# Layer 0's input projection: its last 18 column tiles in nine seven-product pairs behind the attention, and conditioning sums 1024 columns wide

## The chip, the cores and the metric

The kernel runs on one core of one Trainium2 chip. The metric is device time in microseconds (us): the median of three runs of the kernel before is 2300.96 us (2299.42 to 2301.28). One more execution was profiled; all rows shown come from it. Engine names as in the profile: PE is TensorE's matmul, PEld its weight load, DVE is VectorE, ACT is ScalarE, POOL is GpSimd, SP is SyncE, which issues most transfers.

## The reference, cut to what matters

Two transformer layers on 640 tokens (512 latent, 128 context), width 2048, all fp32. Per layer: a conditioning vector (shift, scale, gate) from a small matrix product, RMSNorm, one input projection, mixers, one output projection, gated residual.

```
m = silu(cond) @ ada_w[l] + ada_b[l]           # for c and for c_ctx: two rows, 2048 x 6144 weights
sh, sc, gt = split(m, 3)
h = rms_norm(x, norm_g[l]) * (1 + sc) + sh
# layer 0
qa, ka, va, ga, ub, bb, cb, gb = split_cols(h @ w_in)   # 1024, 256, 256, 1024, 4 x 1024 columns
y_a = banded_attention(q, k, v, sink) * silu(ga)        # 8 heads, 2 key heads
z = cb * ub
conv = zp[:, :-2] * w[0] + zp[:, 1:-1] * w[1] + zp[:, 2:] * w[2]    # depthwise, width 3
y_b = bb * conv * silu(gb)
x = x + gt * (concat([y_a, y_b]) @ w_out)
```

Layer 1 has two dense attention mixers behind its own input projection; the change touches it only through one helper and through the conditioning sums.

## The kernel before, in words

Everything is feature-major: a tile is 128 output columns of a projection by 640 tokens, held as two halves of 320 (`HALF`). The input h stays in SBUF as 16 slabs of 128 features (`hs[k]`), each split in a high and a low part, and so is each weight block (`split_w`, L239 on ACT and L240 on DVE). A product is three matmuls: high by high, high by low, low by high (`proj_q`, L274 to L276). One tile is 4 quarters of k x 2 halves x 4 slabs x 3 = 96 matmuls of 320 columns.

`run_tiles` runs a list of tiles. The first six of layer 0 are led together, while h is made; the others run one by one on two alternating PSUM pairs. Weight quarters are loaded five ahead and split three ahead. After each quarter comes a `slot`: it moves on the generators of `prep` (norms, rotations, gates of finished tiles), those of `attn` (softmax attention of a pair of heads, 11 steps) and, by a credit of `FILL0` per slot, one step of a *fill*.

The fill is `ada_on_dve`: a conditioning block is 512 columns of `ada_w`, summed over 16 blocks of 128 rows. For each, a 256 KB load comes on the SP queue and DVE does two scalar-times-tensor sums of 512 columns (L209, L211), one for each conditioning row. A last fold over the partitions goes through PE, ACT and PE (L217, L220, L223). Layer 0's list does twelve blocks this way; eight more are done on PE before (`ada_on_pe`, L176), four by layer 1's list.

Layer 0 has 52 tiles: q 8, k 2, v 2, attention gate 8, and u, b, c, h (the convolution's input, two factors and gate) 8 each. All 52 are in one list, so attention is spread over the first part of it, and the last 16 tiles are u, c, b, h.

`run_pairs` does two column tiles at once in seven products of half size instead of eight (a Strassen-Winograd form). It needs sums and differences of the halves of the moving operand (`forms`: T2, T3, T4 and T1), made once, and of the four quarters of the weights (operands M1 to M7), made for each pair on DVE. One product is 24 matmuls of 320 columns (L528 to L530). The kernel uses it in both output projections and in a part of layer 1's input projection; `project` runs some single tiles first, and in the last of them the second halves of slabs 0 to 7 are overwritten by T1.

The pools `even` (attention and its work tiles) and `mid` (forms, 8-block weights `w8`, `xr` tiles) share memory. Before, `mid` opens in the middle of the output projection's first tiles, when y is loaded back as its input. The order on each engine is made by the tile framework: it takes instructions in the order of the program as far as their inputs are ready in its own timing.

The softmax (`soft`, L705 to L718) takes the maximum on DVE, the exponential on ACT, the reciprocal on DVE; the weights are scaled on DVE (L798) and transposed on PE (L726).

Of the kernel before, what the change touches and what calls it, by code (L numbers as in the profile page):

```python
# [20 lines left out]
P = 128  # L21
# [28 lines left out]
N_FILL0 = 12  # L50
FILL0 = 1.2
# [5 lines left out]
def trunk_kernel(ctx: ExitStack, tc: tile.TileContext, I: dict, O: dict):  # L57
# [131 lines left out]
    def ada_on_dve(blocks, tags, parts=1, tie=lambda: None):  # L189


        wt, wd = tags[2:5], 512 // parts
        bufs = 3 if wt[0] == wt[1] else 1
        for l, cb in blocks:
            ap = pools["cur"]
            acc = [ap.tile([P, 512], F32, tag=tags[c], name=f"acc{c}", bufs=1) for c in range(2)]
            mark = tie()
            if mark is not None:
                for c in range(2):
                    V.tensor_copy(acc[c][:, 0:1], mark)  # L200
            for i in range(KT * parts):
                kt, h = i % KT, i // KT
                w = ap.tile([P, wd], F32, tag=wt[i % 3], name="adaw", bufs=bufs)
                c0 = cb * 512 + h * wd
                nc.sync.dma_start(w, I["ada_w"][l, kt * P:(kt + 1) * P, c0:c0 + wd])
                for c in range(2):
                    a = acc[c][:, h * wd:(h + 1) * wd]
                    if kt == 0:
                        V.tensor_scalar(a, w, sT[:, kt, c:c + 1], None, ALU.mult)  # L209
                    else:  # L210
                        V.scalar_tensor_tensor(out=a, in0=w, scalar=sT[:, kt, c:c + 1], in1=a,  # L211
                                               op0=ALU.mult, op1=ALU.add)
                yield
            s = psT()
            for g in range(4):
                c, h = g // 2, g % 2
                PE.matmul(s[32 * g:32 * g + 32, 0:256], ones, acc[c][:, h * 256:(h + 1) * 256],  # L217
                          start=True, stop=True, tile_position=(0, 32 * g))
            sb = ap.tile([P, 256], F32, tag=tags[5], name="ada_sb2", bufs=3 if tags[5] == wt[0] else 1)
            A.copy(sb, s[:, 0:256])  # L220
            t = psT()
            for j in range(2):
                PE.transpose(t[:, j * P:(j + 1) * P], sb[:, j * P:(j + 1) * P], ident)  # L223
            t = t[:, 0:256].rearrange("p (j c h x) -> p h j c x", j=2, c=2, h=2)
            for h in range(2):
                add_bias(l, cb, t[:, h, :, :, 0], 2 * h, 2)
            ada_done(l, cb)
            ready.add((l, cb))
            yield

    ready = set()

    def need(l, n, fill):
        while (l, 8 + n // 4) not in ready:
            next(fill)
# [74 lines left out]
    def run_tiles(jobs, w_ap, make_h, fill=None, rate=0.0, ahead=None, order=(0, 1, 2, 3), before=None,  # L310
                  last=None, by_half=False, trans=[], grace=0, cut=None, summed=None, led=None, fill_from=0, lead_in=None, steps=lambda i: 1.0):
# [8 lines left out]
        else:  # L320
# [3 lines left out]
               else new_pp(1 + held.index(n) if trans else n) for n in leads}  # L324
        units = [(pos, qd, js) for pos, qd in enumerate(order) for js in (cut or [(0, 4)])]
        for ui, (pos, qd, js) in enumerate(units if leads else ()):
            queue = nc.gpsimd if trans and ui else None
            raws = {n: load_raw(w_ap, jobs[n][0], qd, js, queue) for n in leads[:W_BUFS]}
            if ui == 0 and lead_in:
                lead_in()  # L330
            parts = {n: split_w(raws[n]) for n in raws}
# [68 lines left out]
        for i in range(lead, len(jobs)):  # L400
            fn = jobs[i][1]
            pp = new_pp((i - lead) % 2)
            split_last = last is not None and i == len(jobs) - 1
# [31 lines left out]
    def run_pairs(cols, w_ap, mov, room, used, begin, done, tail):  # L435
# [82 lines left out]
        for i, (p, name) in enumerate(seq):  # L518
# [25 lines left out]
            if name in ("M7", "M3") and p == len(cols) - 1:  # L544
                tail(name)
# [157 lines left out]
    def soft(ap, width, s, n, rsc, nsink=None, sink=None):  # L703
# [9 lines left out]
        if sink is not None:  # L713
            es = small.tile([P, 1], F32, tag="es", name="es")
            A.activation(es, sink, AF.Exp, bias=nm)
            V.tensor_add(l, l, es)
# [48 lines left out]
    def pair_gen(ap, width, k, v, qs, banded, begin, emit, done, sinks):  # L765
# [27 lines left out]
        def score(u, j):  # L793
            segs, masks, lo, hi, _ = plan(u)
            q = qs[j]
            s = scores(q, u, k, segs, masks)
            p, rl, _ = soft(ap, width, s[:, lo:hi], hi - lo, q[2][u], *sinks[j])
            V.tensor_scalar(p[:, 0:hi - lo], p[:, 0:hi - lo], rl, None, ALU.mult)  # L798
            ps.setdefault(u, []).append(p)
# [35 lines left out]
    ada_rest = [(0, cb) for cb in range(8, 12)] + [(1, cb) for cb in (4, 0, 5, 1, 6, 2, 7, 3, 8, 9, 10, 11)]  # L835
    fill0 = ada_on_dve(ada_rest[:N_FILL0], ("acc0", "acc1", "adaw", "adaw", "adaw", "z"))
    fill1 = ada_on_dve(ada_rest[N_FILL0:], ("acc0", "acc1", "adaw", "adaw", "adaw", "adaw"), 2,
# [125 lines left out]
    def pair_then(width, kk, i, banded, gated):  # L963

        def then():
# [14 lines left out]
            def done():  # L980
                if i in gated:
                    save_y(i, i + 1)
# [4 lines left out]
    def late_gate_job(i, load=False):  # L987
        def f(pp):
            ap = pools["cur"]
            if i < 8 and not load:  # L990
                drain(attn)
            if load and i % 2 == 0:
                y_pair(i)
                for k in (i, i + 1):
                    nc.sync.dma_start(y[k], ydram[k])
# [41 lines left out]
    jobs = []  # L1037

    def b_tiles(i):
        for n, fn in (("u", u_job), ("c", c_job(i)), ("b", b_job(i)), ("h", late_gate_job(8 + i))):  # L1040
            jobs.append((EV[n] + i * P, fn))

    for i in range(4):
        kv, h = i // 2, 2 * i
        if i % 2 == 0:
            jobs.append((EV["k"] + kv * P, k_job("k0", I["cache_a_k"][0, 0, kv], "a_k_norm", O["new_a_k"][0, 0, kv])))
            jobs.append((EV["v"] + kv * P, v_job(I["cache_a_v"][0, 0, kv], O["new_a_v"][0, 0, kv])))
        jobs.append((EV["q"] + h * P, q_job("q0", "a_q_norm")))
        jobs.append((EV["q"] + (h + 1) * P, q_job("q1", "a_q_norm", pair_then(640, "k0", h, True, gated))))
        b_tiles(i)  # L1050
        for j in (h, h + 1):
            jobs.append((EV["g"] + j * P, late_gate_job(j) if i else gate_job(j)))
    for i in range(4, 8):
        b_tiles(i)

    u0, c0, b0, h0, g0, g1 = jobs[4:10]
    jobs[0:10] = [u0, jobs[0], jobs[1], g0, jobs[2], jobs[3], g1, c0, b0, h0]
    run_tiles(jobs, I["ev_w_in"][0], h0_maker, fill0, FILL0, ada_group, trans=TRANS, grace=GRACE, cut=((0, 2), (2, 4)),
              summed=keep, led=even_start, lead_in=lambda: ada_on_pe(0, 0, 0, 2))
    drain(prep)  # L1060
    for _ in fill0:
        pass

# [10 lines left out]
    def forms(src):  # L1074
# [3 lines left out]
        def load(j):  # L1078
            ts = [big("w8", bufs=4)[:, 0:NT] for _ in range(2)]
# [6 lines left out]
        nxt = load(0)  # L1086
        for j in range(8):
            (ya, yb), nxt = nxt, (load(j + 1) if j < 7 else None)
# [18 lines left out]
    def res_load(l, n):  # L1107
        loaded.add((l, n))
        st["xr", n] = pools["cur"].tile([P, NT], F32, tag="xr", name="xr", bufs=3)
# [8 lines left out]
    def late_yin(k):  # L1118
        t = pools["cur"].tile([P, NT], F32, tag="xr", name="yin", bufs=3)
# [10 lines left out]
    def project(w, cols, n0, maker, job, begin, done, tail, n_lead=3, **kw):  # L1130

        go_on = run_tiles([(cols[n], job(n)) for n in range(n_lead)], w, maker, **{"order": (0, 2, 1, 3), **kw})
# [13 lines left out]
        for n in range(n_lead, n0):  # L1146

            used = (n - n_lead) % 2 if n_lead == 3 else 2 if n == n_lead else n % 2
# [60 lines left out]
    make_y0 = y_maker(("q0h", "q0l", "q1h", "q1l"), NT)  # L1209

    def y0_maker(k):
        if k < 4:
            return make_y0(k)
        if k == 8:
            close("even")
            open_pool("mid")
            st["acc"] = pools["cur"].tile([P, NT], F32, name="acc")
            st["sq"] = pools["cur"].tile([P, NT], F32, name="sq")
            attn.append(forms(ydram))
        late_yin(k)  # L1220
# [23 lines left out]
    def norm_half(n, h):  # L1244
# [19 lines left out]
        if h:  # L1264
            st["rbc"] = big("xr", bufs=3)
# [5 lines left out]
    def x1_tail(name):  # L1271

        for i in (range(0, 4) if name == "M7" else range(4, 6)):
# [6 lines left out]
    project_out(0, y0_maker, x1_done, x1_last, x1_tail)  # L1280
# [131 lines left out]
    def gate_out(n):  # L1412
        g = pools["cur"].tile([P, NT], F32, tag="xr", name="g", bufs=3)
# [7 lines left out]
    def value_rows(n, t):  # L1421
        yield
        r = pools["cur"].tile([P, 5, P], F32, tag="xr", name="vr", bufs=3)
# [55 lines left out]
    def very_late_gate(i):  # L1479
        def f(pp):  # L1480
            ap = pools["cur"]
            ti, t, g = (ap.tile([P, NT], F32, tag=tag, name=n, bufs=b)
                        for tag, n, b in (("rp", "yg", 3), ("stg", "gt_t", 2), ("rp", "gg", 3)))
            nc.sync.dma_start(ti, ydram[i])
            for j, sl in HV:
                A.activation(t[:, sl], pp[j][:, 0:HALF], AF.Tanh, scale=0.5)
                V.scalar_tensor_tensor(out=g[:, sl], in0=t[:, sl], scalar=1.0, in1=pp[j][:, 0:HALF],
                                       op0=ALU.add, op1=ALU.mult)
            V.tensor_mul(g, ti, g)
            nc.gpsimd.dma_start(ydram[i], g)  # L1490
        return f

# [21 lines left out]
    for i in (4, 5):  # L1514
        jobs.append((OD["cg"] + i * P, very_late_gate(i)))
# [115 lines left out]
```

## Time and profile before

| | us |
|---|---|
| median of three runs | 2300.96 |
| profiled execution | 2295.65 |
| its span, first to last instruction | 2293.9 |
| PE busy | 2254.7 |
| DVE busy | 1660.4 |
| ACT busy | 1001.3 |
| granted TensorE clock | 0.999 |

Busy is the union of an engine's instructions. A matmul's record is longer than the time to the next one, so PE's pace is read from start to start; DVE's and ACT's instructions overlap a little in the same way. In a row of a group stand the line, engine, operation, tiles out<-in, shapes and count, then busy us and mean ns of one, then the engine's idle time before them and what ended it. In a row in order of time stand the start, the length, engine, line and operation.

### The profile page before, as it was taken

Reading aid. Unit: us, or ns where it says so; the run is one execution under the profiler, and the core shown is the slowest. Engines: PE = TensorE matmul, PEld = TensorE weight load, DVE = VectorE, ACT = ScalarE, POOL = GpSimd, SP = SyncE. Lnnn points to the kernel's source line nnn. Section 1 sums busy time; section 2 is a strip of 40 time slices with the busy share of each in tenths; the row PEclk is TensorE's granted clock in tenths of the full one; section 3 lists DMA queues with packets and bytes.
Section 4 is the critical chain, followed back from the end, with each engine's and each line's share of the span. In section 5 each row is a group of like instructions: output and inputs, shape, how many; then the busy total and the mean of one; then the engine's idle time right before and its main releaser. Section 6 shows DMA issues by size and latency. Waiting matters only on the chain.

```text
span 2293.9 us, 41889 instructions
## 1 busy us (share of the span) xinstructions
PE 2254.7 (98%) x15924; PEld 2183.7 (95%) x15924; DVE 1660.4 (72%) x3327; ACT 1001.3 (44%) x2095; POOL 193.4 (8%) x267
## 2 busy tenths in 40 slices
PE   8999999999999999999999999999999999999999
PEld 5889999999999999999999999999999999999999
DVE  5669887786866663977786665868768778677665
ACT  4335432433422222544654455455555554544343
POOL 2220000000000000000100000100000111111001
PEclk9999999999999999999999999999999999999999
DMA  9984445445455543944673334413324234237541
GB/s 369 330 281 128 151 125 164 139 132 159 127 179 155 153 139 108 288 138 133 228 228 115 116 106 147 137 60 94 111 69 148 73 117 131 77 112 235 159 138 60
DMA packets 398266, 347.54 MB, mean 152 GB/s; under 512 B 19683, under 2 KB 343745, under 8 KB 397553
## 3 DMA queue, kind: packets, MB, share of 16 engines
q1 hardware_dynamic: 384704, 296.19, 42.5%
q0 software_dynamic: 12496, 46.45, 5.4%
q8 instruction: 125, 2.05, 0.4%
q10 hardware_dynamic: 864, 2.23, 0.3%
q14 instruction: 77, 0.62, 0.1%
HBM read 303.89 MB, written 40.90 MB: 150 GB/s over the span
## 4 chain that ended last, share of the span: by engine, by line
PE 85%; DVE 6%; DMA 4%; issue 2%; ACT 2%; POOL 1%; SPq 0%; POOLq 0%; ACTq 0%; DVEq 0%
PE pa L274 8%; PE pb L274 8%; PE pb L275 8%; PE pb L276 8%; PE pa L275 8%; PE pa L276 8%; PE pq L530 7%; PE pq L529 7%; PE pq L528 7%; PE T L726 2%; PE S L738 1%; PE T L176 1%; DMA adaw<-in_ada_w 1%; PE S L740 1%; PE S L739 1%
## 5 line engine op out<-in xcount | busy, mean ns | idle before, releaser
L239 ACT ACTIVATE wh<-raw 128x512 fp32r<-128x512 f32 (+1 forms) x454 | 275.7, 608 | 659.6 <-PE pb L275 546.8
L274 PE MATMUL pa<-h,wh 128*128 128x320 f32 x1504 | 477.3, 317 | 2.4 <-ACT h L239 1.8
L275 PE MATMUL pa<-h,wh 128*128 128x320 f32 x1504 | 467.2, 311 | 1.3 <-DVE h L240 1.1
L274 PE MATMUL pb<-h,wh 128*128 128x320 f32 x1504 | 466.8, 311 | 0.9 <-ACT h L239 0.9
L276 PE MATMUL pb<-h,wl 128*128 128x320 f32 x1504 | 466.5, 310 | 0.0
L276 PE MATMUL pa<-h,wl 128*128 128x320 f32 x1504 | 466.2, 310 | 0.0
L275 PE MATMUL pb<-h,wh 128*128 128x320 f32 x1504 | 465.7, 310 | 0.0
L240 DVE TENSOR_TENSOR wl<-raw,wh 128x512 fp32r<-128x512 f32 (+1 forms) x454 | 299.6, 660 | 226.2 <-ACT wh L239 210.1
L211 DVE SCALAR_TENSOR_TENSOR acc<-adaw,sT,acc 128x512 f32<-128x512 f32 (+1 forms) x600 | 359.6, 638 | 12.0 <-DMA adaw<-in_ada_w 11.6
L274 PEld LDWEIGHTS pa<-h,wh 128*128 128x128 f32 x1504 | 282.8, 188 | 13.9 <-issue 10.0
L275 PEld LDWEIGHTS pa<-h,wh 128*128 128x128 f32 x1504 | 283.1, 188 | 6.2 <-issue 3.7
L276 PEld LDWEIGHTS pa<-h,wl 128*128 128x128 f32 x1504 | 282.5, 188 | 2.9 <-issue 2.9
L274 PEld LDWEIGHTS pb<-h,wh 128*128 128x128 f32 x1504 | 283.0, 188 | 2.1 <-ACT h L239 1.1
L275 PEld LDWEIGHTS pb<-h,wh 128*128 128x128 f32 x1504 | 282.9, 188 | 0.4 <-issue 0.4
L276 PEld LDWEIGHTS pb<-h,wl 128*128 128x128 f32 x1504 | 282.9, 188 | 0.4 <-issue 0.4
L528 PE MATMUL pq<-h,wh 128*128 128x320 f32 x608 | 188.6, 310 | 0.0
L530 PE MATMUL pq<-h,wl 128*128 128x320 f32 x608 | 188.1, 309 | 0.2 <-DVE wl L240 0.2
L529 PE MATMUL pq<-h,wh 128*128 128x320 f32 x608 | 187.8, 309 | 0.0
L712 ACT ACTIVATE p<-S,nm,rq 128x768 f32<-128x768 f32 (+3 forms) x120 | 101.3, 844 | 101.1 <-DVE nm L707 69.4
L528 PE MATMUL pq<-T,wh 128*128 128x320 f32 x456 | 141.8, 311 | 0.1
L530 PE MATMUL pq<-T,wl 128*128 128x320 f32 x456 | 141.0, 309 | 0.2 <-DVE wl L240 0.2
L529 PE MATMUL pq<-T,wh 128*128 128x320 f32 x456 | 141.0, 309 | 0.0
(344 smaller groups left out, 3938.4 us busy)
## 6 DMA issues: line engine op xcount, KB each, us to landing
adaw<-in_ada_w SPq DMA_DIRECT2D x192, 256.0 KB, 2.9
raw<-in_ev_w_in SPq DMA_DIRECT2D x184, 256.0 KB, 2.9
raw<-in_od_w_in SPq DMA_DIRECT2D x160, 256.0 KB, 2.9
ada<-in_ada_w SPq DMA_DIRECT2D x11, 2048.0 KB, 13.1
adaw<-in_ada_w SPq DMA_DIRECT2D x128, 128.0 KB, 2.2
w<-in_od_w_in SPq DMA_DIRECT2D x24, 512.0 KB, 3.9
adah<-in_ada_w SPq DMA_DIRECT2D x20, 512.0 KB, 9.1
yd<-y POOLq DMA_DIRECT2D x32, 320.0 KB, 3.3
```

Source lines behind the costliest of these rows:

```text
L176: PE.matmul(acc[32 * g:32 * g + 32, 0:wd], sT[:, kt, :], w[:, kt % m, :], start=(i < 4), stop=(i >= KT - 4), tile_position=(0, 32 * g))
L211: V.scalar_tensor_tensor(out=a, in0=w, scalar=sT[:, kt, c:c + 1], in1=a, op0=ALU.mult, op1=ALU.add)
L239: A.activation(hi, x, AF.Copy)
L240: V.tensor_sub(lo, x, hi)
L274: PE.matmul(ps, wh[:, i, :], hi[:, sl], start=(j == js[0] if alone else (pos == 0 and j == 0)), stop=False)
L275: PE.matmul(ps, wh[:, i, :], lo[:, sl], start=False, stop=False)
L276: PE.matmul(ps, wl[:, i, :], hi[:, sl], start=False, stop=(j == js[1] - 1 if alone else (pos == 3 and j == 3)))
L528: PE.matmul(ps, wh[:, j, :], hi, start=(first and h == 0 and j == 0), stop=False, skip_group_check=True)
L529: PE.matmul(ps, wh[:, j, :], lo, start=False, stop=False, skip_group_check=True)
L530: PE.matmul(ps, wl[:, j, :], hi, start=False, stop=(final and h == 1 and j == 3), skip_group_check=True)
L712: A.activation(p[:, 0:n], s, AF.Exp, scale=rsc, bias=nm, accum_out=l)
L726: PE.transpose(t[:, i * P:(i + 1) * P], p, ident)
```

## The change

- Layer 0's list is reordered and cut. 28 tiles come first: all of q, k, v, the first four attention gates, u, c, b, h of groups 0 to 2. Then come four attention gates, u and c of group 3 (six single tiles), then nine pairs: (b, h) of group 3, and (u, c) and (b, h) of groups 4 to 7.
- At the 29th tile (`tail_turn`) the attention and the fill are run out, `even` closes and `mid` opens; from there `forms(None)` makes the forms from h itself (high plus low). In the last single tile the second halves run first, and `twist` then overwrites those of slabs 0 to 7 with T1.
- Gates 2 to 7 load y back from scratch memory, multiply and store it; attention stores every pair of heads.
- The convolution of the later groups runs without padding, in one tile.
- The output projection's first four slabs and two weight quarters are loaded during the last pair.
- Five twins of conditioning blocks are summed 1024 columns at a time from 512 KB loads (`ada_wide`), one sum per step at 2.05 steps per slot; two blocks go to PE, two matmuls of 512 columns per step (`ada_beside`), behind the turn. Layer 1's list does its four blocks as before.
- The softmax weights of banded and plain attention are scaled on ACT.

```
-N_FILL0 = 12
-FILL0 = 1.2
+FILL0 = 2.05
...
+    def ada_wide(twins):
+        for l, cb in twins:
+            ap = pools["cur"]
+            acc = [ap.tile([P, 1024], F32, tag=f"acc{c}", name=f"acc{c}", bufs=1) for c in range(2)]
+            for kt in range(KT):
+                w = ap.tile([P, 1024], F32, tag="adaw", name="adaw", bufs=3)
+                nc.sync.dma_start(w, I["ada_w"][l, kt * P:(kt + 1) * P, cb * 512:(cb + 2) * 512])
+                for c in range(2):
+                    if kt == 0:
+                        V.tensor_scalar(acc[c], w, sT[:, kt, c:c + 1], None, ALU.mult)
+                    else:
+                        V.scalar_tensor_tensor(out=acc[c], in0=w, scalar=sT[:, kt, c:c + 1], in1=acc[c],
+                                               op0=ALU.mult, op1=ALU.add)
+                    yield
+            for b in range(2):
+                ada_fold(l, cb + b, [a[:, b * 512:(b + 1) * 512] for a in acc], ap, "z", 1)
+                yield
+    def ada_beside(blocks):
+        for l, cb in blocks:
+            acc = pS.tile([P, 1024], F32, tag="S", name="adaS")
+            for k0 in range(0, KT, 2):
+                w = big("w8", bufs=4).rearrange("p (k n) -> p k n", k=2)
+                nc.sync.dma_start(w, ada_src(l, cb, k0, 2))
+                yield
+                for kt in (k0, k0 + 1):
+                    g = kt % 4
+                    PE.matmul(acc[32 * g:32 * g + 32, 0:512], sT[:, kt, :], w[:, kt % 2, :],
+                              start=(kt < 4), stop=(kt >= KT - 4), tile_position=(0, 32 * g))
+            sb = big("w8", bufs=4)
+            A.copy(sb[:, 0:512], acc[:, 0:512])
+            yield
+            tr = psT()
+            for j in range(4):
+                PE.transpose(tr[:, j * P:(j + 1) * P], sb[:, j * P:(j + 1) * P], ident)
...
+            if turn and i == turn[0]:
+                drain(prep)
+                fill = turn[1]()
+                rate = turn[2]
...
+            if twist and i == len(jobs) - 1:
+                for hv in (HV[1:], HV[:1]):
+                    for qd in range(4):
+                        proj_q(pp, parts[t + qd], qd, qd, hv)
+                        run_ahead(t + 1)
+                        slot(fill, rate / 2, steps(i) / 2)
+                    if hv[0][0]:
+                        twist()
...
-            V.tensor_scalar(p[:, 0:hi - lo], p[:, 0:hi - lo], rl, None, ALU.mult)
+            A.activation(p[:, 0:hi - lo], p[:, 0:hi - lo], AF.Copy, scale=rl)
...
+    fill0 = ada_wide([(0, 8), (1, 4), (1, 0), (1, 6), (0, 10)])
+    fill0b = ada_beside([(1, 2), (1, 3)])
...
+    jobs = [u0, k0, v0, g0, q0, q1, g1, c0, b0, h0, q2, q3, u1, c1, b1, k1, v1, q4, q5, h1, u2, c2, q6, q7, b2, h2, g2, g3]
+    n_turn, last_q = len(jobs), jobs.index(q7)
+    for j in range(4, 8):
+        jobs.append((EV["g"] + j * P, very_late_gate(j, (("xr", 5),) * 3)))
...
+    def tail_turn():
+        drain(attn)
+        for _ in fill0:
+            pass
+        close("even")
+        open_pool("mid")
+        st["acc"], st["sq"] = (pools["cur"].tile([P, NT], F32, tag=n, name=n) for n in ("acc", "sq"))
+        attn.append(forms(None))
+        return fill0b
+    def twist():
+        drain(attn)
+        for _ in fill0b:
+            pass
+        for j in range(8):
+            hi, lo = hs[j]
+            split(hi[:, HALF:NT], lo[:, HALF:NT], t1[j])
...
+                     steps=lambda i: 0.4 if i >= n_turn else 1.35 if i > last_q else 1.0,
+                     turn=(n_turn, tail_turn, 1.0), twist=twist)
+    tails = [("b", "h", 3)] + [x for i in range(4, 8) for x in (("u", "c", i), ("b", "h", i))]
...
+    run_pairs([(EV[a] + i * P, EV[b] + i * P) for a, b, i in tails], I["ev_w_in"][0],
+              {"B11": half_of(0, 0), "T1": half_of(0, 1), "B21": half_of(8, 0), "B22": half_of(8, 1),
+               "T2": form_of(0), "T3": form_of(1), "T4": form_of(2)}, room, used, tail_begin, tail_done, tail_tail)
```

235 lines of the change are left out of this document (143 added, 92 removed).

## The prediction

> **What bounds the kernel now.** I read the page's head and chain first, then busy time by stage, then single instructions in order of time on TensorE and on VectorE, then VectorE's groups and waits in the stage that the change rewrites.
>
> ```profile
> span 2293.9 us, 41889 instructions
> ...
> PE 2254.7 (98%) x15924; PEld 2183.7 (95%) x15924; DVE 1660.4 (72%) x3327; ACT 1001.3 (44%) x2095; POOL 193.4 (8%) x267
> ...
> PE 85%; DVE 6%; DMA 4%; issue 2%; ACT 2%; POOL 1%; SPq 0%; POOLq 0%; ACTq 0%; DVEq 0%
> ```
>
> TensorE (PE) is busy 98% of the span and holds 85% of the chain that ended last, so matmuls taken out should come off the time if the other engines keep pace. Whether they do is a question by stage. Columns below: stretch in us, its length, then busy us (count) of PE, weight loads, VectorE (DVE), ScalarE (ACT), GpSimd.
>
> ```profile
> 158.00:905.00 747.00, 745.08 (x5255) 727.94 (x5254) 546.74 (x1078) 256.05 (x554) 25.58 (x29) 1.00 0.48 143
> 905.00:980.00 75.00, 72.09 (x477) 69.58 (x476) 63.44 (x107) 37.47 (x60) 2.71 (x5) 1.00 0.86 270
> 980.00:1110.00 130.00, 130.00 (x888) 130.00 (x888) 100.32 (x160) 59.08 (x101) 5.40 (x10) 1.00 0.45 131
> ```
>
> ```profile
> 200.00:240.00 40.00, 39.94 (x301) 38.32 (x300) 38.69 (x91) 18.08 (x42) 0.60 (x1) 1.00 0.46 134
> ...
> 587.00:636.00 49.00, 49.00 (x366) 47.81 (x365) 46.47 (x109) 20.23 (x50) 0.00 (x0) 1.00 0.53 158
> ```
>
> The first row is layer 0's input projection behind its six leading tiles: 46 tiles. PE idles 2 us there, DVE is busy 73%. The third is the existing seven-product loop in the output projection: PE full, DVE 77%. The last two, of a finer division, are attention stretches: DVE at 97% and 95%, and PE still full.
>
> **Terms on TensorE.**
>
> ```profile
> 699.96 0.31 PE L274 MATMUL pa<-h,wh 128*128 128x320 f32 x1
> ...
> 703.33 0.31 PE L276 MATMUL pb<-h,wl 128*128 128x320 f32 x1
> 703.57 0.64 PE L217 MATMUL T<-acc,ones 128*32 128x256 f32 x8
> 704.14 0.42 PE L274 MATMUL pa<-h,wh 128*128 128x320 f32 x1
> 704.39 0.31 PE L275 MATMUL pa<-h,wh 128*128 128x320 f32 x1
> ```
>
> ```profile
> 129.31 1.93 PE L176 MATMUL T<-ada,sT 128*32 128x256 f32 x32
> 131.17 0.41 PE L274 MATMUL pa<-h,wh 128*128 128x320 f32 x1
> ```
>
> ```profile
> 987.46 0.31 PE L528 MATMUL pq<-T,wh 128*128 128x320 f32 x1
> ...
> 990.98 0.31 PE L528 MATMUL pq<-h,wh 128*128 128x320 f32 x1
> ```
>
> A matmul of 320 columns lasts 0.31 us but the next starts 0.147 us later: 699.96 to 703.33 is 23 steps in 3.37 us. A product of a pair is 24 such matmuls: 987.46 to 990.98, 3.52 us, the same 0.147.
>
> 1. *Pairs.* Two tiles cost 192 matmuls, a seven-product pair 7 x 24 = 168. Nine pairs drop 9 x 24 = 216, at 0.147: **-31.8 us**.
>
> 2. *Two conditioning blocks on TensorE* (`ada_beside`). From 703.33 to 704.39 pass 1.06 us, where two plain steps take 0.29: one group of column-tiled matmuls with 256 fp32 columns (`ada_on_dve` issues four matmuls, recorded as 8) costs 0.77. Four such groups (129.31 to 131.17) take 1.86 against 0.57 for one (703.57 to 704.14), so a further group is 0.43, and going into that shape and back is the other 0.34. The new matmuls are 512 columns wide; no row shows that width, and I take twice 0.43 = 0.86. The generator yields after every two matmuls, and at rate 1.0 one such step stands in each slot with 12 to 24 ordinary matmuls between: two blocks x 8 steps = 16 insertions of 0.86 + 0.34 = 1.20: 19.2 us. Lower end: each block's 16 matmuls run together as four full groups, 2 x (4 x 0.86 + 0.34) = 7.6 us. I take 19.2, since the slots keep them apart. Each block also has four transposes of 128 columns; none should cost more than a 320-column step, so eight lie between 0 and 1.2, and I take 0.6. **+19.8 us**, lower end +8.
>
> 3. *Folds.* Ten blocks keep the old fold on PE; two lose it, 0.77 each and two transposes at the 0.07 just taken: **-1.8 us**. The 1024 columns change nothing on PE.
>
> Sum on PE: -31.8 + 19.8 - 1.8 = **-13.8 us**.
>
> **Terms that must stay hidden on VectorE.** The change packs twelve blocks' worth of summing, less two, from 46 tiles into the 22 before the turn.
>
> ```profile
> L211 DVE SCALAR_TENSOR_TENSOR acc<-adaw,sT,acc 128x512 f32<-128x512 f32 x360 | 254.6, 745 | 5.4 <-DMA adaw<-in_ada_w 5.2
> L240 DVE TENSOR_TENSOR wl<-raw,wh 128x512 fp32r<-128x512 f32 x180 | 123.9, 688 | 125.4 <-ACT wh L239 119.1 <-PE T L558 5.6
> ...
> L1022 DVE SCALAR_TENSOR_TENSOR cv<-z,vec,cv 128x642 f32<-128x642 f32 x16 | 14.1, 883 | 0.1
> ...
> L798 DVE TENSOR_SCALAR p<-p,rl 128x640 f32<-128x640 f32 x16 | 8.8, 550 | 0.2
> L798 DVE TENSOR_SCALAR p<-p,rl 128x512 f32<-128x512 f32 x16 | 7.7, 484 | 0.2
> ```
>
> ```profile
> 304.12 0.74 DVE L211 SCALAR_TENSOR_TENSOR acc<-adaw,sT,acc 128x512 f32<-128x512 f32 x1
> 304.78 0.42 DVE L240 TENSOR_TENSOR ptl<-T,pth 128x256 fp32r<-128x256 f32 x1
> ```
>
> ```profile
> 992.48 1.23 DVE L470 TENSOR_TENSOR sx<-sx,w 128x1024 f32<-128x1024 f32 x1
> 993.63 0.82 DVE L1227 TENSOR_TENSOR acc<-acc,sq 128x640 f32<-128x640 f32 x1
> ```
>
> Back to back, instructions overlap by about 0.08: the 512-wide sum costs 0.66 (304.12 to 304.78), a 1024-wide add 1.15 (992.48 to 993.63). The sum at 512 is 0.05 dearer than an add, so I estimate 1.20 at 1024. New stage, g1 to g3, 22 tiles:
> - PE: 747 less 24 tiles x 96 x 0.147 = 339, less two folds: **406 us**.
> - DVE: 547, less 360 x 0.66 + 24 x 0.4 = 247 of old sums, less 24 x 4 splits x 0.61 = 59, less 16 for the softmax scaling that goes to ACT, less some 35 (an estimate: five convolution groups and their gates, the L1022 row and its neighbours in kind), plus five twins x (30 x 1.20 + 2 x 0.67) = 187: **377 us**, 93% of 406.
>
> The rows at 95% and 97% lost nothing, but they had slack on both sides, and here there is none for 400 us. I take **+4 us**; below nothing it can't go, since DVE ahead of PE gives PE nothing; the upper end is the first rival.
>
> The Trainium skill, "Perfetto Trace Analysis", section "Optimizing Scalar/DVE Operations", says a DVE instruction on SBUF carries about 60 ns of engine time that grouping saves when the engine is full. By that, an estimate from the page's figure, the 150 merged sums would save 9 us instead of the 18 that 2 x 0.66 - 1.20 gives, and DVE would need 386 in the stage, 95%: nearer to the first rival, on the same side.
>
> *Edits at about nothing.* Softmax scaling on ACT: 0.5 to 1 us each, 40 times in each layer; ACT is busy 44% of the span (the page's second row above), so it has room; a later scaling delays transposes, a freer DVE helps: -3 to +3. Forms from the resident h (eight adds, subtractions and splits, some 35 us of DVE) lie under six tiles of 14.1 us in which DVE has no sums; if that cover went, the twist would wait. The pair loop's operand sums lie beside PE as in the 980 to 1110 row. Wider transfers: 512 KB instead of 256 KB on the SP queue, about one per slot, ahead of the weight loads; the stage's mean of 143 GB/s would be about 200. Pairs load the same bytes of weights as the tiles they replace. Heads 2 to 7 are now saved ungated, reloaded for their gate and saved again: six more saves on the POOL queue and six more loads on SP, 320 KB each, with a tile's time of 14 us to land; behind a late y load only a gate waits, and no matmul until two tiles on. *Hand-over* to the output projection: the 905 to 980 row shows 2.9 us idle, part of which earlier loads of weights and y may remove; the turn and the twist may cost as much. 0, between -3 and +6.
>
> Total: -13.8 + 4 = **-9.8 us**. The profiled execution took 2295.65 us (span 2293.9 and 1.8 around it), 5.3 below the median of 2300.96. So 2285.9 against its own time, **2291 us** on the median's scale (-0.4%).
>
> **Rivals.**
>
> ```profile
> DVE acc L209 <- PE T L217: 15.6, 8, 2.9
> ...
> DVE l L716 <- ACT es L715: 10.6, 13, 1.3
> ...
> DVE qsw L648 <- ACT qsw L647: 5.3, 6, 2.0
> DVE acc L211 <- DMA adaw<-in_ada_w: 5.2, 7, 1.4
> DVE gg L1000 <- ACT gt_t L999: 5.0, 5, 1.0
> ```
>
> *VectorE becomes the bound before the turn (slower).* These are DVE waits of the old stage that no order of work removes; these five make 41.7 us, and with the smaller ones I put them at 50 to 58. Were they all kept, the stage would need 377 + 55 = 432 against 406: +26, in all +12: **2313 us**. The sign turns when the stage passes 420 us, DVE under 90% busy. For it: the wait on the fold (15.6) comes once per twin with one accumulator buffer, and nothing later makes up lag. Against: the attention rows, where such waits were filled at 95 to 97%. Chance 0.20.
>
> *The wide sums hold up what is urgent.* A softmax or split instruction that arrives behind a sum waits up to 1.2 us instead of 0.66, on average 0.27 more; four DVE steps in each of 40 scores: 43 us of delay, mostly covered by the slots between. A quarter of it on PE would be +11, **2300 us**, no change. The same section of the Trainium skill says that where an engine isn't saturated but causes bubbles elsewhere, instructions are better broken up; no row here shows that. Chance 0.10.
>
> *The insertions are cheap.* The matmuls of several steps run together, or fill idle PE time: -11.6 from term 2's lower end, **2279 us**. For it: the x8 and x32 rows run four column groups at once, and a step of two leaves half of them empty. Against: one step per slot. Chance 0.13.
>
> **Numbers.** The forecast (2291, its own range 2284 to 2298) has 0.57. Low 2275: the cheap insertions without the 4 us. High 2308: most of the first rival; about 0.1 lies on either side. A measurement tells some 0.2%, 4.6 us, from no change. Faster by more: 0.51 of the forecast's 0.57 and the cheap insertions' 0.13, 0.64. Slower: 0.18 of the first rival, 0.02 of the second and 0.01 of the forecast, 0.21. Within: 0.15.
>
> **What would show it.** Nine pairs at 24.7 us each, back to back, where 18 tiles took 14.1 each. Sixteen column-tiled insertions behind the turn, each about 1.05 us from start to the next plain matmul and 1.2 dearer than none. The turn at about 158 + 410 = 568 us. DVE at 90 to 95% in the 22 tiles, PE idle there under 8 us. What would make it wrong: PE waiting for weight splits or softmax before the turn; PE idle at the twist or where y comes back; insertions of another price.

## The result, and the profile after

The changed kernel took 2296.14 us (median, 2293.2 to 2300.56), the kernel before on the same chip 2299.51 us (2295.94 to 2302.1): a ratio of 0.9987, 95% interval 0.998 to 0.9994. It is faster by some 3 us (0.13%), which is less than the 0.2% the prediction called measurable at all. The forecast was -9.8 us; its own range, 2284 to 2298, holds the median near its upper edge. That it lies inside is owed more to the width of the range than to the sum: by stage, the terms below miss by 9 us in all. The profiled execution took 2295.01 us, 0.6 less than that of before.

The head of the page after, its chain, and the group of the wide sums (count, busy us, mean ns, idle before):

```profile
span 2293.2 us, 41410 instructions
...
PE 2245.8 (98%) x15760; PEld 2156.4 (94%) x15760; DVE 1685.5 (73%) x3188; ACT 1109.8 (48%) x2269; POOL 196.1 (9%) x273
...
PE 84%; DVE 7%; DMA 4%; ACT 2%; issue 2%; POOL 1%; SPq 0%; ACTq 0%; POOLq 0%; DVEq 0%
...
L245 DVE SCALAR_TENSOR_TENSOR acc<-adaw,sT,acc 128x1024 f32<-128x1024 f32 x150 | 188.5, 1276 | 0.0
```

PE is busy 8.9 us less (2254.7 before), and the span is only 0.7 us shorter: PE lost work and stood idle instead. DVE's share of the chain went from 6% to 7%. The page can't say where, so the span is cut at single instructions found in the rows in order of time: the first sum that ACT takes from the six led tiles, the gate of the last of the 22 tiles ahead of the turn, the first and last matmul of the pairs, the first of the projection's pairs, and the last matmul of layer 1's norm.

| stage, us | before | after | forecast |
|---|---|---|---|
| to the end of the led tiles | 158.0 | 160.6 | 158.0 |
| 22 tiles to the last gate | | 417.3 | 410 |
| six tiles with the insertions | | 104.2 | 104.4 |
| nine pairs | | 221.4 | 222.3 |
| these three (46 tiles before) | 746.9 | 743.0 | 737 |
| to the projection's pairs | 60.1 | 56.4 | 60.1 |
| projection's pairs and layer 1's norm | 156.1 | 154.5 | 156.1 |
| layer 1 from there to the end | 1172.8 | 1178.7 | 1172.8 |
| span | 2293.9 | 2293.2 | 2284 |

Against the forecast: +2.6 in the led tiles, +5.9 in the rebuilt stage, -3.7 and -1.6 at the hand-over, +5.9 in layer 1. Together +9.1, which turns -9.8 into -0.7.

Busy time by stage of the changed kernel (stretch, length, then busy us and count of PE, weight loads, DVE, ACT, POOL; then granted clock, DMA share, GB/s):

```profile
160.60:200.00 39.40, 35.81 (x247) 34.21 (x246) 31.57 (x52) 19.94 (x50) 3.92 (x4) 1.00 0.65 204
200.00:240.00 40.00, 37.34 (x262) 34.21 (x261) 37.93 (x68) 21.79 (x46) 2.08 (x2) 1.00 0.48 145
160.60:577.90 417.30, 409.97 (x2933) 389.63 (x2932) 362.48 (x618) 208.53 (x465) 25.03 (x26) 1.00 0.56 171
577.90:682.10 104.20, 103.57 (x645) 86.97 (x645) 64.40 (x110) 31.14 (x53) 2.69 (x5) 1.00 0.60 188
682.10:905.00 222.90, 222.90 (x1523) 222.90 (x1522) 169.58 (x260) 101.33 (x177) 2.17 (x4) 1.00 0.35 105
905.00:975.00 70.00, 70.00 (x480) 70.00 (x479) 58.90 (x101) 33.85 (x56) 2.69 (x5) 1.00 0.81 249
```

The pairs and the hand-over run without a gap. Of the 7.3 us that PE stands idle in the 22 tiles, 6.3 lie in the first 80 us (3.6 and 2.7 in the first two rows). The 22 tiles took 11 us more than the forecast's 406 of PE alone; the other 4 are PE's own busy time, 410.0 in the row, and no run takes them apart. DVE, over the whole stretch, is busy 87%.

### The profile page after: what moved, and what is told of

Read it like the earlier page. It is cut to its first block, busy times and chain, and to the rows that moved or that the text cites. A ratio compares the mean times of both kernels' runs of the same rounds, so it can differ in the third digit from the quotient of the medians.

```text
span 2293.2 us, 41410 instructions
## 1 busy us (share of the span) xinstructions
PE 2245.8 (98%) x15760; PEld 2156.4 (94%) x15760; DVE 1685.5 (73%) x3188; ACT 1109.8 (48%) x2269; POOL 196.1 (9%) x273
## 4 chain that ended last, share of the span: by engine, by line
PE 84%; DVE 7%; DMA 4%; ACT 2%; issue 2%; POOL 1%; SPq 0%; ACTq 0%; POOLq 0%; DVEq 0%
PE pq L583 10%; PE pq L584 10%; PE pq L582 10%; PE pa L313 6%; PE pa L314 6%; PE pb L314 6%; PE pb L313 6%; PE pa L315 6%; PE pb L315 6%; PE T L780 2%; DMA adaw<-in_ada_w 2%; PE S L792 1%; DVE acc L210 1%; PE S L794 1%; PE S L793 1%
## 5 line engine op out<-in xcount | busy, mean ns | idle before, releaser
L313 PE MATMUL pa<-h,wh 128*128 128x320 f32 x1216 | 389.4, 320 | 0.6 <-DVE z L1064 0.4
L314 PE MATMUL pa<-h,wh 128*128 128x320 f32 x1216 | 380.1, 313 | 1.4 <-DVE h L279 1.4
L313 PE MATMUL pb<-h,wh 128*128 128x320 f32 x1216 | 378.2, 311 | 0.9 <-ACT h L278 0.9
L315 PE MATMUL pb<-h,wl 128*128 128x320 f32 x1216 | 377.8, 311 | 0.0
L314 PE MATMUL pb<-h,wh 128*128 128x320 f32 x1216 | 377.7, 311 | 0.0
L582 PE MATMUL pq<-h,wh 128*128 128x320 f32 x896 | 277.2, 309 | 0.0
L584 PE MATMUL pq<-h,wl 128*128 128x320 f32 x896 | 276.9, 309 | 0.0
L583 PE MATMUL pq<-h,wh 128*128 128x320 f32 x896 | 276.8, 309 | 0.0
L313 PEld LDWEIGHTS pa<-h,wh 128*128 128x128 f32 x1216 | 229.3, 189 | 22.6 <-ACT wh L278 9.2
L314 PEld LDWEIGHTS pa<-h,wh 128*128 128x128 f32 x1216 | 229.7, 189 | 6.5 <-issue 4.5
L313 PEld LDWEIGHTS pb<-h,wh 128*128 128x128 f32 x1216 | 229.0, 188 | 3.3 <-issue 1.2
L314 PEld LDWEIGHTS pb<-h,wh 128*128 128x128 f32 x1216 | 229.1, 188 | 1.7 <-issue 1.7
L582 PE MATMUL pq<-T,wh 128*128 128x320 f32 x672 | 208.0, 309 | 0.0
L583 PE MATMUL pq<-T,wh 128*128 128x320 f32 x672 | 207.6, 309 | 0.0
L245 DVE SCALAR_TENSOR_TENSOR acc<-adaw,sT,acc 128x1024 f32<-128x1024 f32 x150 | 188.5, 1276 | 0.0
L278 ACT ACTIVATE wh<-sx 128x512 fp32r<-128x512 f32 x168 | 105.6, 633 | 147.8 <-PE pq L583 100.0
```

The lines of the kernel that those rows point to most:

```text
L245: V.scalar_tensor_tensor(out=acc[c], in0=w, scalar=sT[:, kt, c:c + 1], in1=acc[c], op0=ALU.mult, op1=ALU.add)
L278: A.activation(hi, x, AF.Copy)
L313: PE.matmul(ps, wh[:, i, :], hi[:, sl], start=(j == js[0] if alone else (pos == 0 and j == 0)), stop=False)
L314: PE.matmul(ps, wh[:, i, :], lo[:, sl], start=False, stop=False)
L315: PE.matmul(ps, wl[:, i, :], hi[:, sl], start=False, stop=(j == js[1] - 1 if alone else (pos == 3 and j == 3)))
L582: PE.matmul(ps, wh[:, j, :], hi, start=(first and h == 0 and j == 0), stop=False, skip_group_check=True)
```

## The experiments

In each diff, `-` is the changed kernel unless another is named. Medians of one group are against one median of the kernel before on the same chip: 2300.56 us for e1 to e4, 2300.19 us for e8 to e11. These medians differ by about 1 us from chip to chip, so two edits of different groups are compared by their ratios to the kernel before, where the changed kernel's is 0.9987.

### What an insertion costs: steps of four matmuls (e1_quads)

```diff
-            for k0 in range(0, KT, 2):
-                w = big("w8", bufs=4).rearrange("p (k n) -> p k n", k=2)
-                nc.sync.dma_start(w, ada_src(l, cb, k0, 2))
-                yield
-                for kt in (k0, k0 + 1):
+            for k0 in range(0, KT, 4):
+                ws = []
+                for k in (k0, k0 + 2):
+                    ws.append(big("w8", bufs=4).rearrange("p (k n) -> p k n", k=2))
+                    nc.sync.dma_start(ws[-1], ada_src(l, cb, k, 2))
+                    yield
+                for kt in range(k0, k0 + 4):
...
```

> The two conditioning blocks on TensorE are issued four matmuls at a time (all four column groups) in 8 steps instead of two at a time in 16. Theory (an insertion costs 0.86 of stream and 0.34 of going into that shape and back, whether two or four column groups run): 8 insertions of 1.2 us fewer, the stretch from the turn to the first pair shrinks from 104.9 to about 95.3 us, the kernel is 9 to 10 us faster than the changed one, about 2286. Rival (the price goes by the matmul, so that four cost twice what two cost): the same 104.9 us, 2296.

Measured: 2289.35 us, ratio 0.9949 (0.9932 to 0.9966), 0.0038 or some 8.7 us better than the changed kernel's. PE in order of time, one insertion of the changed kernel (start, length, line, operation; a record x4 is two matmuls):

```profile
594.27 0.31 PE L315 MATMUL pb<-h,wl 128*128 128x320 f32 x1
594.51 1.05 PE L262 MATMUL adaS<-w,sT 128*32 128x512 f32 x4
595.49 0.41 PE L313 MATMUL pa<-h,wh 128*128 128x320 f32 x1
595.74 0.30 PE L314 MATMUL pa<-h,wh 128*128 128x320 f32 x1
```

and one of e1_quads, with four matmuls:

```profile
598.92 0.31 PE L317 MATMUL pb<-h,wl 128*128 128x320 f32 x1
599.16 1.07 PE L264 MATMUL adaS<-w,sT 128*32 128x512 f32 x8
600.15 0.41 PE L315 MATMUL pa<-h,wh 128*128 128x320 f32 x1
600.40 0.30 PE L316 MATMUL pa<-h,wh 128*128 128x320 f32 x1
```

From the last plain matmul to the second one behind pass 1.47 us in the one (594.27 to 595.74) and 1.48 in the other, where two plain steps take 0.29. So an insertion costs 1.18 and 1.19: two further column groups cost 0.01. What is paid is the insertion, not the matmul. All of them cost the same but the first of each kernel, which also waits for its weights (1.88 and 2.14). With eight instead of sixteen the stretch from the last gate to the pairs shrank by 9.0 us, near 8 x 1.18 = 9.4:

```profile
579.90:675.10 95.20, 95.20 (x646) 86.11 (x645) 64.39 (x110) 30.98 (x53) 2.70 (x5) 1.00 0.64 206
```

### Where the 22 tiles lose: sums that begin later (e3_late_sums)

The sums begin three tiles (12 weight quarters) later and then go at a higher rate.

```diff
-FILL0 = 2.05
+FILL0 = 2.35
...
-                     cut=((0, 2), (2, 4)), summed=keep, led=even_start, lead_in=lambda: ada_on_pe(0, 0, 0, 2),
+                     cut=((0, 2), (2, 4)), summed=keep, led=even_start, lead_in=lambda: ada_on_pe(0, 0, 0, 2), fill_from=12,
```

> The wide sums start 12 slots later, when the keys, values and queries of the leading tiles are through, and go at 2.35 steps per slot instead of 2.05. Theory (the 22 tiles before the turn lost about 7 us beyond the forecast in their first 60 us, where key and query work stands behind wide sums and their first load): lead end to turn falls from 417 us to 409 to 412, the kernel is 5 to 8 us faster, about 2290. Rival (VectorE is short over the whole stage, and the same work in fewer slots loses elsewhere what it gains at the start): 415 to 420 us, 2294 to 2298.

Measured: 2290.77 us, ratio 0.9961 (0.9946 to 0.9976), 0.0026 or some 6 us better than the changed kernel's. Busy time by stage of e3_late_sums:

```profile
161.30:200.00 38.70, 37.20 (x257) 34.98 (x256) 31.26 (x60) 23.06 (x58) 5.68 (x5) 1.00 0.59 189
200.00:240.00 40.00, 40.00 (x295) 38.62 (x294) 38.95 (x71) 23.63 (x50) 0.60 (x1) 1.00 0.53 154
161.30:572.10 410.80, 408.70 (x2932) 389.89 (x2931) 361.52 (x618) 208.99 (x464) 25.32 (x26) 1.00 0.58 174
```

The stage takes 410.8 us, 6.5 less, with the same 618 instructions on DVE; PE's idle time in the first two stretches falls from 6.3 to 1.5 us. The difference is no accident of one execution: the five other profiles that begin the same wide sums early take 417.4 to 419.5 us here, e10_best below, which begins them late, 411.0. So the loss was not a lack of room on DVE. What it was, DVE in order of time in the changed kernel shows (in brackets the idle time before, and what ended it):

```profile
165.40 0.69 DVE L279 TENSOR_TENSOR wl<-raw,wh 128x512 fp32r<-128x512 f32 x1 [0.68 <-ACT wh L278]
168.52 0.75 DVE L243 TENSOR_SCALAR acc<-adaw,sT 128x1024 f32<-128x1024 f32 x1 [2.42 <-DMA adaw<-in_ada_w]
169.19 0.68 DVE L648 TENSOR_TENSOR kg<-T,gain_rows 128x512 f32<-128x512 f32 x1
```

and PE beside it:

```profile
167.47 0.31 PE L315 MATMUL pb<-h,wl 128*128 128x320 f32 x1
169.93 0.44 PE L676 MATMUL T<-ident,ctxk 128*128 128x128 f32 x2 [2.14 <-DVE kg L648]
```

The first sum stands in DVE's queue ahead of `kg` and waits 2.42 us for its 512 KB; `kg`, behind it, holds PE's transposes for 2.14 us. In e3_late_sums `kg` starts at 166.97 and no sum stands before it:

```profile
166.13 0.69 DVE L279 TENSOR_TENSOR wl<-raw,wh 128x512 fp32r<-128x512 f32 x1 [3.93 <-ACT wh L278]
166.97 0.69 DVE L648 TENSOR_TENSOR kg<-T,gain_rows 128x512 f32<-128x512 f32 x1
```

A second such place, sums and no load, is PE's wait of 1.97 us at 211 us, for a weight split behind two sums:

```profile
209.92 1.27 DVE L245 SCALAR_TENSOR_TENSOR acc<-adaw,sT,acc 128x1024 f32<-128x1024 f32 x1
211.12 0.15 DVE L770 TENSOR_TENSOR l<-l,es 128x1 f32<-128x1 f32 x1
211.19 1.27 DVE L245 SCALAR_TENSOR_TENSOR acc<-adaw,sT,acc 128x1024 f32<-128x1024 f32 x1
212.39 0.15 DVE L772 RECIPROCAL rl<-l 128x1 f32<-128x1 f32 x1
212.46 0.67 DVE L279 TENSOR_TENSOR wl<-raw,wh 128x512 fp32r<-128x512 f32 x1
```

The split's input was ready from 210.8, when ACT had finished its `wh`; it starts at 212.46. The wait is gone in e3_late_sums, which at 200 to 240 has PE full. The two places are 4.1 of the 7.3 us.

### How near DVE is to the bound: sums of 512 columns (e11_narrow)

The loads stay 512 KB; each sum is done as two halves.

```diff
-                    if kt == 0:
-                        V.tensor_scalar(acc[c], w, sT[:, kt, c:c + 1], None, ALU.mult)
...
+                    for b in range(2):
+                        a, x = acc[c][:, b * 512:(b + 1) * 512], w[:, b * 512:(b + 1) * 512]
+                        if kt == 0:
+                            V.tensor_scalar(a, x, sT[:, kt, c:c + 1], None, ALU.mult)
...
```

> The wide loads stay, but each sum of 1024 columns is two of 512: 150 more sums, 18 us more of VectorE before the turn by 2 x 0.66 - 1.20. Theory (VectorE is about full in that stage, so what is added there goes to the end): lead end to the last gate before the turn grows from 417 to 430 to 436 us, the kernel to 2308 to 2315. Rival (there is cover, or long instructions hold up urgent ones and short ones help): 410 to 421 us, 2290 to 2300.

Measured: 2303.88 us, ratio 1.0018 (1.0007 to 1.0028). The 22 tiles of e11_narrow:

```profile
161.80:584.80 423.00, 414.29 (x2933) 392.00 (x2932) 381.32 (x778) 209.30 (x465) 26.16 (x26) 1.00 0.56 169
```

160 instructions more cost DVE 18.8 us (381.32 less 362.48), 0.12 each, and the stage 5.7 us (3.5 against the slowest of the profiles with wide sums): at most 0.3 us for each us of DVE. DVE took up the rest in its idle time, which fell from 54.8 to 41.7 us. Neither theory holds outright: a stage bound by DVE would have paid it all, one with room nothing. Nor is it a full test of shorter instructions, since both halves are issued in the same step: ahead of the same split now stand four half sums (213.34 to 216.12) where two sums stood. It also shows what the wide sums are worth: without them the change would have been slower than the kernel before.

### The softmax scaling (e2_scale_l0, e4_before_scale)

e2_scale_l0 puts it back on DVE in layer 1:

```diff
-            A.activation(p[:, 0:hi - lo], p[:, 0:hi - lo], AF.Copy, scale=rl)
+            if banded:
+                A.activation(p[:, 0:hi - lo], p[:, 0:hi - lo], AF.Copy, scale=rl)
+            else:
+                V.tensor_scalar(p[:, 0:hi - lo], p[:, 0:hi - lo], rl, None, ALU.mult)
```

> The softmax scaling stays on ScalarE in layer 0 and goes back to VectorE in layer 1. Theory (layer 1's attention list took 4.8 us more in the changed kernel's profile, 598.7 against 593.9, because the scaling on ScalarE reorders the work there): the list is back at 592 to 595 us, the kernel 4 to 5 us faster than the changed one, about 2292. Rival (the longer list is chance or comes from elsewhere, as no scaling is done after 1750 us where most of the loss stands): 597 to 600 us, 2296.

Measured: 2298.6 us, ratio 0.9991 (0.9982 to 1.0), and layer 1 from its norm 1180.7 us: no gain. The theory that the scaling alone slows layer 1 falls.

e4_before_scale is the kernel before with that one line of the change:

```diff
-            V.tensor_scalar(p[:, 0:hi - lo], p[:, 0:hi - lo], rl, None, ALU.mult)
+            A.activation(p[:, 0:hi - lo], p[:, 0:hi - lo], AF.Copy, scale=rl)
```

> The kernel before with one part of the change alone: the softmax scaling of banded and plain attention on ScalarE. Theory (as for the layer 0 only kernel): layer 1's list grows by 3 to 6 us, layer 0's tiles stay within 1 us, in all 2302 to 2305. Rival (moving it costs nothing, the prediction's term of -3 to +3 around nothing): 2298 to 2301.

Measured: 2302.67 us, ratio 1.0012 (1.0002 to 1.0021): alone it costs 2 to 3 us (2.1 between the medians, 2.8 by the ratio), inside the -3 to +3 that the prediction gave it and against the rival that it costs nothing. Layer 1's attention list (first to last score matmul) takes 596.0 us instead of 593.9, less than the theory's 3 to 6 more.

### Layer 1's order: the carried fractions (e8_carry, e9_carry_l0, e12_after_again, e13_before_again)

Two counters, `credit` (steps of the fill) and `pace` (steps of attention), keep their fractions between slots, and nothing resets them between the layers. The kernel before enters layer 1's list with 0.8 and 0.0, the changed one with 0.4 and 0.2, since layer 0's rates and slots changed. So layer 1, which the diff hardly touches, gets its sums and attention steps in other slots. e8_carry sets the old values; e9_carry_l0 also has the edit of e2_scale_l0.

```diff
+CARRY = 0.8, 0.0
...
+    credit[0], pace[0] = CARRY
     run_tiles(jobs, I["od_w_in"][0], None, fill1, FILL1, fill_from=FILL1_FROM,
```

> The changed kernel, with one line ahead of layer 1's attention list that sets the two fractions which slots carry over (the fill's credit and attention's pace) to what they are there in the kernel before, 0.8 and 0.0; the changed kernel arrives with 0.4 and 0.2. No work is added or left out. Theory (these fractions shift the sums and the attention steps by a slot and so reorder layer 1's list, which took 599 to 602 us in every changed kernel against 594): the list comes back to 594 to 597 us (596 in the kernel before with the scaling on ScalarE), the kernel gains 3 to 5 us on the changed one, 2291 to 2293. Rival (the list is longer for another cause, such as five buffers in place of three or where things lie in SBUF): 599 to 602 us, 2296.

> As the carry kernel, and the softmax scaling on ScalarE in layer 0 alone: layer 1's instructions then stand on TensorE in exactly the order of the kernel before. Theory: 593 to 595 us for layer 1's list, 2290 to 2292 in all. Rival (order isn't the cause): 599 us, 2296 to 2298.

Measured: 2294.2 us, ratio 0.9978 (0.9967 to 0.9988), and 2294.6 us, ratio 0.9977 (0.9967 to 0.9987). Against the changed kernel's 0.9987 that is some 2 us, with intervals that overlap, and less than the 3 to 5 and 4 to 6 expected.

To see how much belongs to one execution, both kernels were profiled once more, with nothing edited.

> The changed kernel once more, nothing edited; asked is how much of layer 1's 5.9 us (from the end of its norm to the end of the span: 1172.8 before, 1178.7 after) belongs to the program and how much to one execution. Theory (the order of layer 1's list, given by the fractions carried into it): the same instructions wait at the same places again, so the list (first to last score matmul) takes 598 to 599 us and norm to end 1178 to 1179. Rival (falls of the granted clock, which come in some executions and cost about 1.7 us each): the list comes out at 595 to 597 in an execution without a fall in layer 1.

> The kernel before once more, nothing edited, beside the run above. Theory: the list takes 593 to 595 us and norm to end 1172 to 1174 again. Rival: its first profile was a lucky execution, and the list comes out at 596 or more, within 2 us of the changed kernel's.

Measured: 2301.06 and 2298.42 us, one execution each, and from layer 1's norm to the end 1181.5 and 1173.2. The kernel before repeats itself; the changed one is longer still than its theory said. The rival's condition, an execution without a fall of the clock in layer 1, was not met: this profile has one fall too, and so has every other with a list near 600. But one fall, worth some 1.5 us (last section), can't make the 7 us between the two lists. Layer 1's list by stretch (columns as above), one row for each kernel; before, then e13_before_again:

```profile
1476.50:2070.40 593.90, 581.85 (x4110) 561.52 (x4108) 450.01 (x1032) 313.81 (x714) 62.35 (x68) 1.00 0.33 102
```

```profile
1479.70:2073.90 594.20, 581.91 (x4110) 561.49 (x4108) 449.57 (x1031) 313.57 (x715) 61.83 (x68) 1.00 0.34 101
```

the changed kernel, then e12_after_again:

```profile
1471.10:2069.80 598.70, 584.38 (x4111) 563.39 (x4110) 431.61 (x994) 341.41 (x755) 61.02 (x68) 1.00 0.33 101
```

```profile
1474.00:2075.20 601.20, 584.30 (x4110) 563.25 (x4109) 431.54 (x993) 341.49 (x755) 60.91 (x68) 1.00 0.33 100
```

e8_carry, then e9_carry_l0:

```profile
1471.00:2068.10 597.10, 583.47 (x4111) 562.04 (x4110) 432.62 (x994) 341.50 (x755) 61.39 (x68) 1.00 0.34 101
```

```profile
1472.40:2068.50 596.10, 582.75 (x4111) 561.72 (x4110) 450.89 (x1034) 314.08 (x715) 62.38 (x68) 1.00 0.33 101
```

The loss belongs to the program: 593.9 and 594.2 against 598.7 and 601.2, with the same 4110 matmuls. The five profiles with the changed kernel's fractions (it, its repeat, e1, e2, e11) have lists of 598.7, 601.2, 601.3, 599.0 and 599.2, on average 599.9; the three with the old fractions (e8, e9 and the last kernel below) 597.1, 596.1 and 595.8, on average 596.3. e3_late_sums, at its other rate, arrives with fractions of its own, 0.6 and 0.2, and takes 602.0. So the fractions cost layer 1 about 4 us in the profiles, of which the medians show 2 at best. The last 2 us to the kernel before stay open, and PE's order is not their cause: e9_carry_l0 and the last kernel have the list's matmuls in exactly the order of the kernel before and still take 596.1 and 595.8.

### All four together (e10_best)

The edits of e1_quads, e3_late_sums, e2_scale_l0 and e8_carry at once.

> Four edits together: steps of four conditioning matmuls, the wide sums 12 slots later at 2.35 per slot, the scaling on ScalarE in layer 0 alone, the fractions set back. If they add up: 6.8 (steps of four) + 5.4 (late sums) + 4 to 5 (layer 1's order) below the changed kernel's 2296, 2278 to 2281, 0.8 to 0.9% under the kernel before. If the gains overlap (the clock's short falls, which cost where TensorE idles, are part of each): 2282 to 2286.

Measured: 2276.96 us (four runs, 2276.21 to 2283.27), ratio 0.9905 (0.9888 to 0.9921), faster than both kernels. Its stages up to the pairs and its list in layer 1:

```profile
160.80:571.80 411.00, 408.76 (x2933) 389.93 (x2932) 361.63 (x618) 208.95 (x465) 25.53 (x26) 1.00 0.58 174
571.80:667.30 95.50, 95.22 (x645) 86.04 (x645) 64.41 (x110) 30.93 (x53) 2.71 (x5) 1.00 0.65 205
1456.30:2052.10 595.80, 582.35 (x4110) 561.66 (x4109) 450.49 (x1032) 313.73 (x715) 62.38 (x68) 1.00 0.34 101
```

Each part nearly keeps what it had alone: 6.3 us in the 22 tiles, 8.7 in the six tiles, and the list at 596. Layer 1's norm ends 14.4 us earlier than in the changed kernel (1100.1 against 1114.5), and the rest takes 4.4 less (1174.3 against 1178.7): the 18.8 us between the spans, 2293.2 and 2274.4. By the ratios, the single edits e1, e3 and e8 (0.0038, 0.0026 and 0.0009 below 0.9987) add up to 0.9914, inside the interval of the 0.9905 measured: the parts add up within the noise.

## Why the prediction was right or wrong

- **Pairs, -31.8.** Right. They take 24.6 us each, without a gap, where 24.7 was forecast.
- **Blocks on TensorE, +19.8.** Right, and for the reason given: the price goes by insertions, sixteen of them, 1.18 each where 1.20 was taken. The first also waits 0.63 us for its weights. The rival of cheap insertions was false as the kernel stands: the sixteen steps stayed apart. Its premise, that a step of two leaves half of the column groups empty, is what e1_quads uses.
- **Cover on VectorE, +4.** This step failed, in size and in kind. The 22 tiles took 417.3 us, 11 above the 406 of PE alone instead of 4. The prediction looked for the cause in DVE's total (377 us estimated, 93%). DVE was busy 362.5, 87%, and PE lost most in the first 80 us, where a sum at the head of DVE's queue waited for its load and two sums stood ahead of a split. e3_late_sums, with the same work in another order, lands on 410.8. That this is the forecast's own 410 is partly luck: its 4.8 us above 406 are 2.1 of idle time and 2.7 of busier PE. PE's idle time, 7.3 us, was inside the "under 8" and so no warning; the turn was late all the same (578 against 568), partly from the 2.6 us of the led tiles.
- **First rival (VectorE the bound).** It was to decide from 420 us on, with DVE under 90%; the stage came to 417 at 87%, near its mark. But e11_narrow, with 18.8 us more on DVE, lost 5.7 at most, so DVE was not the bound throughout. Nor were the rival's five waits, 41.7 us before, such that no order of work removes them: in the 22 tiles the sum's wait for its load (L211 before, L245 after) no longer stands among DVE's waits, and the other four come to 11.1 us (total, times, longest):

```profile
DVE l L770 <- ACT es L769: 3.5, 6, 0.9
DVE acc L243 <- PE T L221: 3.4, 2, 3.1
...
DVE qsw L702 <- ACT qsw L701: 2.6, 3, 1.6
...
DVE gg L1241 <- ACT gt_t L1240: 1.6, 2, 1.0
```

- **Second rival (wide sums hold up urgent work).** The mechanism is there (the split at 212.46 behind two sums), but halving the sums within a step made it worse, by up to 5.7 us. (The forecast's 2300 for it is a round figure: 11 us on PE give 2298 in place of the 4 and 2302 beside them.) In the Trainium skill, "Perfetto Trace Analysis", section "Optimizing Scalar/DVE Operations", breaking up instructions that cause bubbles elsewhere, on an engine that isn't saturated, may let work be completed sooner. e11_narrow doesn't bear that out here; beginning the sums later was the remedy, and finer steps were not tried. The 60 ns for an instruction on SBUF in that section of the Trainium skill also falls short: the prediction's rows gave 0.12 us for each merged pair of sums, and e11_narrow measured 0.12.
- **Scaling on ACT, 0.** Alone it cost 2 to 3 us (e4_before_scale); in the changed kernel its place in layer 1 made no difference that these runs tell (e8_carry against e9_carry_l0).
- **Hand-over, 0.** Better than taken: -3.7 us to the projection's pairs, of which 2.9 is the idle time of before that is gone; and -1.6 up to layer 1's norm, not followed up.
- **Left out.** Layer 1 was put at nothing, beyond the scaling, because the diff hardly touches it. It cost 5.9 us in the first pair of profiles and 8.3 in the second (1181.5 against 1173.2), about 4 of it by the order that the carried fractions set, as e8_carry and e9_carry_l0 show in their profiles, and the rest is open. The led tiles cost 2.6 us: the same three loads of 2 MB take 10.4 us instead of 9.3 to land, and PE waits 1.5 us for one at 135. Every profile of the changed kernel and its variants has it (159.8 to 163.2 against 158.0 to 158.7); why is open.

So the direction and the terms on PE were right. What PE waits for was not: 5.9 us in the rebuilt stage (7.3 in the 22 tiles, less what the six tiles and the pairs took below their forecast), 5.9 in layer 1 and 2.6 in the led tiles came back, and the stretches from the pairs to layer 1's norm gave 5.3.

## What to carry to other kernels

When work is packed into a stage, its share on the helping engine says little: look at the first instruction of the packed work in that engine's queue, which load it waits for, and which urgent instruction stands behind it; beginning it three tiles later saved 6.5 us here and cost nothing that the stage shows. Small matmuls of another tile shape are paid by the insertion, so fill all column groups in each. Counters that carry fractions from one stage to the next make any change of rates a change of order in all later stages: reset them, and compare stages that the diff doesn't touch.

## What the hardware showed that was not expected

PE's clock falls to half for 3.4 us at some places where PE had been idle for about 2 us. PE in order of time, in the changed kernel:

```profile
1936.09 0.38 PE L676 MATMUL T<-ident,ctxk 128*128 128x128 f32 x2
1938.38 0.66 PE L612 MATMUL T<-ident,m 128*128 128x128 f32 x4 [1.91 <-DVE m L668]
...
1941.09 0.47 PE L313 MATMUL pa<-h,wh 128*128 128x320 f32 x1
1941.36 0.47 PE L314 MATMUL pa<-h,wh 128*128 128x320 f32 x1
...
1943.32 0.31 PE L313 MATMUL pb<-h,wh 128*128 128x320 f32 x1
1943.47 0.31 PE L314 MATMUL pb<-h,wh 128*128 128x320 f32 x1
```

and the stretch with its granted clock, 0.76:

```profile
1937.00:1944.00 7.00, 5.62 (x28) 5.53 (x29) 4.31 (x10) 2.47 (x7) 0.00 (x0) 0.76 0.36 103
```

After an idle time of 1.91 us the step of a 320-column matmul is 0.27 us instead of 0.147 until 1943: 3.4 us at that pace lose some 1.5 us. So an idle time near 2 us can cost nearly twice its length. It doesn't always: the 2.14 us at 168 brought no fall. But the early waits of the 22 tiles do bring one or two, between 170 and 217 us, in six of the seven profiles that begin the sums early (all but the changed kernel's own), and none in e3_late_sums and e10_best. Between the falls at layer 1's norm and at the last matmuls, which all profiles have, the five with the changed kernel's fractions have eight, six of them inside the list, e3_late_sums has two, and the six others (before, its repeat, e4, e8, e9, e10) have none. The idle times at the start of these ten were 1.9 to 3.0 us. Six of 1.5 us over five profiles are 1.8 us: half of the 3.6 us between the two averages above. In the Trainium skill, "TensorE: Matmul & The Clock Gate", section "What's actually happening", the clock goes to half after an idle window of about 3.4 us, in windows that run freely. The length of the falls agrees; the idle time ahead of this one was shorter.
